# Up-projection start of a two-layer trunk: three chunks by halves of tokens in place of four, block 3's last steps by halves, and a moved weight split

## The chip, the cores and the metric

The kernel runs on one core of one Trainium2 chip. The metric is device time in microseconds (us) of one execution. TensorE is called PE here, VectorE DVE, ScalarE ACT, GpSimd POOL and SyncE SP, as in the profile.

## The reference, cut to what matters

The trunk has two layers on a residual stream `h` of 512 tokens by 1024 features, in float32. Each layer is a mixer (windowed attention in layer 0, forgetting attention in layer 1) and a ConvFFN, each with a norm before and a norm after. The change lies where the mixer's result is added and the ConvFFN begins:

```python
def rms_norm(x, g):
    x32 = x.astype(jnp.float32)
    y = x32 * lax.rsqrt(jnp.mean(x32 * x32, axis=-1, keepdims=True) + EPS)
    return (y * g.astype(jnp.float32)).astype(x.dtype)

def conv_ffn(xn, w_up, cw, cb, w_down):
    a = xn @ w_up                                   # 512 x 1024 by 1024 x 5632
    ap = jnp.pad(a, ((0, 0), (CONV_W - 1, 0), (0, 0)))
    a = sum(ap[:, j:j + T] * cw[j] for j in range(CONV_W)) + cb
    gate, val = jnp.split(a, 2, axis=-1)
    return (jax.nn.gelu(gate, approximate=True) * val) @ w_down
...
    h = h + rms_norm(mix, g[1])
    f = conv_ffn(rms_norm(h, g[2]), w_up[l], conv_w[l], conv_b[l], w_down[l])
    h = h + rms_norm(f, g[3])
```

## The kernel before, in words

**Precision.** Every product of a weight and an activation is made of three matmuls: each operand is split into a high part, rounded to the matmul's input type, and a low part, the difference. `mm3` (L290) issues high by high, high by low, low by high; these are the lines L291, L292 and L293 of the profile. Each has 128 rows of features on the partitions and 512 or 256 tokens as columns.

**Weights.** The class `Weights` brings the weights in pieces of 128 x 1024 through raw buffers. `load` issues the DMA on SP. `high` copies the piece to its high part on ACT (L60), `low` subtracts that from the raw piece on DVE (L78). `get` hands out the next piece and first splits ahead, up to `W.ahead` pieces counting from the one handed out. A few pieces are split in another way, with a DMA that adds (`high_added`, L98). As every engine works through its instructions in program order, the place at which a split is called is its place in the queues of ACT and DVE, and the place of the load it asks for in SP's.

**Order.** The schedule is written out by hand: an engine's order is the program's order, and waits between engines come from the data and the buffers. Eight PSUM banks are shared by everything that PE writes.

**The boundary.** The tokens lie in four blocks of 128. `Proj.finish` ends the mixer's projection block by block, in two halves of 512 features. After each half `Mix.part` squares the result on ACT (L333), multiplies it by its gain on DVE (L340), and after the second half takes the root. `Mix.add` (L342) takes the reciprocal and adds the block to `h` on DVE (L347). `Boundary.norm` then normalises `h`: `rstd_h` squares a whole block on ACT (L298), takes the root (L300) and the reciprocal (L304), and `normed` makes `xn` in two halves on DVE (L312). `transpose_in` transposes `xn` on PE in two groups of four (L362), ACT casts each group to the high part (L369), DVE makes the low part (L370). Blocks 0 and 1 pass through these steps inside the projection; `first_products` does block 3's norm and the transposes of blocks 2 and 3.

**The up-projection's start.** A chunk is 128 of the 5632 up-projected features; its weight is one piece. `first_products(bd, 4)` takes four chunks. The low half of the tokens (`LO`, blocks 0 and 1) of each is multiplied first, and between these products stand the transposes of block 2 (behind chunk 0) and block 3 (behind chunk 2). Then come the high halves (`HI`) of all four. Splits of three further pieces are called from here: ahead of chunks 1, 2 and 3, as `W.ahead` is 4 and four pieces are split at the start.

**After it.** `sums_in` prepares sums and differences of the transposed activations: two additions of 128 x 2048 on POOL (L670), called right behind `first_products`, then subtractions on DVE (L672 to L676) and splits on ACT and DVE (L681, L682). `post(0, ...)` and `post(1, ...)` do the convolution's taps of chunks 0 to 3, as pairs 0 and 1 (ACT L635, DVE L636 and L638), the gate (ACT L656) and the product of gate and value (DVE L653). The number in `post` and in the later loop counts pairs of a gate chunk and a value chunk. Pairs 2 and 3 go through `up`, with all 512 tokens in one matmul. From pair 4 on, most pairs are multiplied by a scheme with seven products of half size (`SEVEN`), which uses `sums_in`'s results; in it DVE reads a PSUM bank (L978, L982) before PE adds the next product to that bank. In layer 0, three small operations on DVE for a later gate weight (L1492 to L1494) stand between the end of `finish` and block 3's norm.

Of the kernel before, what the change touches and what calls it, by code (L numbers as in the profile page):

```python
# [11 lines left out]
BF16 = mybir.dt.bfloat16  # L12
AF = mybir.ActivationFunctionType
ALU = mybir.AluOpType

D = 1024
T = 512
NB = 4
KD = D // 128
# [3 lines left out]
EPS = 1e-6  # L23
# [94 lines left out]
def trunk_kernel(ctx, tc, x, norm_gains, w_qkv_a, w_o_a, w_q_b, w_o_b, kv_norm, w_kvf, b_f,  # L118
                 w_up, conv_w, conv_b, w_down, rope, out):
    nc = tc.nc  # L120
    act, dve, pool, pe, sp = nc.scalar, nc.vector, nc.gpsimd, nc.tensor, nc.sync
# [8 lines left out]
    def t8(shape, dt=F32, name="t8"):  # L130
        return p8.tile(shape, dt, tag="t8", name=name)

    def t4(shape, dt=F32, name="t4"):
        return p4.tile(shape, dt, tag="t4", name=name)

    def t2(shape, dt=F32, name="t2"):
        return p2.tile(shape, dt, tag="t2", name=name)

    def bank(shape, name="bank"):
        return psp.tile(shape, F32, tag="ps", name=name)  # L140

    def small(n, name):
        return sml.tile([128, n], F32, tag=name, name=name)
# [73 lines left out]
    W = Weights(nc, new_raw, lambda: t8([128, 2, 1024], F32R, name="w"), pieces)  # L217
# [4 lines left out]
    h = cst.tile([128, NB, D], F32, name="h")  # L222
# [6 lines left out]
    def load_gain(src, name):  # L229
        t = t4([128, D], name=name)  # L230
        sp.dma_start(t, bass.AP(tensor=src.tensor, offset=src.offset, ap=[[0, 128], [1, D]]))
        return t
# [57 lines left out]
    def mm3(o, ah, al, bh, bl, first, last, shared=False):  # L290
        pe.matmul(o, ah, bh, start=first, stop=False, skip_group_check=shared)  # L291
        pe.matmul(o, ah, bl, start=False, stop=False, skip_group_check=shared)  # L292
        pe.matmul(o, al, bh, start=False, stop=last, skip_group_check=shared)  # L293

    def rstd_h(b, between=None):
        ss = small(1, "s1")
        junk = t2([128, D], BF16, name="junk")
        act.activation(junk, h[:, b, :], AF.Square, scale=1.0 / 32, accum_out=ss)  # L298
        sd = small(1, "sd")
        act.activation(sd, ss, AF.Sqrt, bias=eps_t)  # L300
        if between is not None:
            between()
        r = small(1, "rs")
        dve.reciprocal(r, sd)  # L304
        return r

    H2 = (slice(0, 512), slice(512, 1024))

    def normed(b, r, gain):
        xn = t4([128, D], name="xn")  # L310
        for s, g in zip(H2, gain):
            dve.scalar_tensor_tensor(xn[:, s], h[:, b, s], r, g, ALU.mult, ALU.mult)  # L312
        return xn

    def by_half(gain):
        return [gain[:, s] for s in H2]

    class Mix:
# [5 lines left out]
        def half(self, b, n, hf, o):  # L324
            self.part(b, n, o, H2[hf], n == 1)
# [46 lines left out]
    def xs(xT, kc, s):  # L372
        return xT[0][kc // 4][:, kc % 4, s], xT[1][kc // 4][:, kc % 4, s]


    def feat_mm(w, xT, o, s):
        wh, wl = (t.rearrange("p (k c) -> p k c", k=8) for t in w)
        for kc in range(KD):
            bh, bl = xs(xT, kc, s)
            mm3(o[:, s], wh[:, kc, :], wl[:, kc, :], bh, bl, kc == 0, kc == KD - 1)  # L380
# [53 lines left out]
    class Boundary:  # L434
# [11 lines left out]
        def half(self, i, n, hf, o):  # L446
            b = self.order[i]
            self.mix.half(b, n, hf, o)
            if n == 0:
                if i >= 2:  # L450
                    self.transpose(self.order[i - 2])
                if i >= 1:
                    self.norm(self.order[i - 1])
            else:
                self.mix.add(b)

        def norm(self, b):
            self.r[b] = rstd_h(b)
            self.xn[b] = normed(b, self.r[b], by_half(self.gain_next))

        def transpose(self, b):
# [85 lines left out]
    def first_products(bd, n):  # L547
        bd.norm(3)
        outs = [bank([128, T], name="first") for _ in range(n)]
        ws = []  # L550
        for i, o in enumerate(outs):
            ws.append(W.get())
            feat_mm(ws[i], bd.xT, o, LO)
            if i == 0:
                bd.transpose(2)
            if i == 2:
                bd.transpose(3)
        for w, o in zip(ws, outs):
            feat_mm(w, bd.xT, o, HI)
        return outs  # L560
# [65 lines left out]
    def ffn(l, bd, cp, nxt, ahead):  # L626
# [39 lines left out]
        def sums_in():  # L666

            v = [t8([128, 4, T], name=f"xsum{i}") for i in range(2)]
            for i in range(2):
                pool.tensor_tensor(v[i], xT[0][i].bitcast(F32), xT[1][i].bitcast(F32), ALU.add)  # L670
            yield
            dve.tensor_tensor(v[0][:, :, LO], v[0][:, :, HI], v[0][:, :, LO], ALU.subtract)  # L672
            dve.tensor_tensor(v[0][:, :, HI], v[1][:, :, HI], v[0][:, :, HI], ALU.subtract)
            yield
            dve.tensor_tensor(v[1][:, :, HI], v[1][:, :, HI], v[0][:, :, LO], ALU.subtract)
            dve.tensor_tensor(v[1][:, :, LO], v[1][:, :, LO], v[1][:, :, HI], ALU.subtract)  # L676
            yield
            for X, src in ((XA, v[0]), (XB, v[1])):
                X += [t8([128, 4, T], F32R, name="xsh"), t8([128, 4, T], F32R, name="xsl")]
                for k in (0, 2):  # L680
                    act.copy(X[0][:, k:k + 2], src[:, k:k + 2])  # L681
                    dve.tensor_tensor(X[1][:, k:k + 2], src[:, k:k + 2], X[0][:, k:k + 2].bitcast(F32), ALU.subtract)  # L682
                    yield
# [250 lines left out]
        def up(w, o, kcs):  # L934
            wh, wl = (t.rearrange("p (k c) -> p k c", k=8) for t in w)
            for kc in kcs:
                bh, bl = xs(xT, kc, ALL)
                mm3(o, wh[:, kc, :], wl[:, kc, :], bh, bl, kc == 0, kc == KD - 1)

        base = W.n_get  # L940
        first = first_products(bd, 4)
        xT = bd.xT
        extra = sums_in()
        next(extra)
        post(0, first[0:2])
# [8 lines left out]
        for c in range(2, NF):  # L954
# [68 lines left out]
            else:  # L1023
                banks = [bank([128, T], name="up") for _ in range(1 if begun else 2)]
                if begun:
                    w, first = begun
# [165 lines left out]
    sd = tc.dram_tile([T, 8], F32, name="sd")  # L1192
# [291 lines left out]
    bd = Boundary(load_gain(norm_gains[0, 1], "gain01"), load_gain(norm_gains[0, 2], "gain02"), "xb")  # L1484
# [13 lines left out]

    bd2 = SharedBoundary(load_gain(norm_gains[0, 3], "gain03"), gcol, "xk")
    ffn(0, bd, cp[0], bd2, 4)  # L1500


# [67 lines left out]
    first, second = bd2.order[:2], bd2.order[2:]  # L1570
# [212 lines left out]
    for n in range(N + 3):  # L1783
        live = n < N
        if live:
            j, i = units[n]
# [51 lines left out]
    bd = Boundary(load_gain(norm_gains[1, 1], "gain11"), load_gain(norm_gains[1, 2], "gain12"), "xc")  # L1838
    po.finish(bd, 4)


    ffn(1, bd, cp, Final(load_gain(norm_gains[1, 3], "gain13")), 0)


# [40 lines left out]
```

## Time and profile before

| what | value |
|---|---|
| median of three runs | 1099.43 us (1098.59 to 1100.11) |
| the profiled execution's own time | 1098.99 us |
| its span, first to last instruction | 1097.2 us |
| mean granted clock of PE | 0.999 |
| PE busy | 1089.6 us, 99% |
| DVE busy | 878.0 us, 80% |
| ACT busy | 668.9 us, 61% |
| POOL busy | 175.9 us, 16% |

The profile is of one execution. A row of a timeline has the start in us from the span's start, the duration in us, the engine, the line of the kernel, the operation, the tiles written and read, shapes and types, and the count of instructions put together; in brackets stands how long the engine sat idle just before it, and what released it. A matmul's duration reaches over those that follow it, so PE's pace is read from the distance of starts. Rows of waits have the sum in us, the number of times and the longest.

In layer 0 the four chunks run from 173.18 to 197.93 us, in layer 1 from 751.98 to 776.73 us.

### The profile page before, as it was taken

What the parts mean: (1) busy time and instruction counts of PE and PEld (TensorE: products, weight loads), DVE (VectorE), ACT (ScalarE), POOL (GpSimd) and SP (SyncE); (2) the same over time, 40 slices, a digit from 0 to 9 for tenths busy, and PEclk for the clock granted to TensorE, in tenths of its full rate; (3) what the DMA queues carried; (4) which work ended last, traced back from release to release, by engine and by line L of the source; (5) the groups of instructions that cost most, each with busy time, mean ns of one, the idle gap of its engine ahead of it and who ended that gap; (6) DMA issues with size and microseconds to landing.
All of it is one profiled execution on the core that took longest, in us unless ns stands there. A gap on an engine that the chain in (4) does not pass through costs nothing.

```text
span 1097.2 us, 18058 instructions
## 1 busy us (share of the span) xinstructions
PE 1089.6 (99%) x6592; PEld 949.0 (86%) x6592; DVE 878.0 (80%) x1498; ACT 668.9 (61%) x1114; POOL 175.9 (16%) x245
## 2 busy tenths in 40 slices
PE   9999999999999999999999999999999999999997
PEld 7988889899999988888878888889899999988886
DVE  5898978887878689897686667858888778689894
ACT  6754665756666756576451577755756666647572
POOL 3633002211111111000001212101311111211000
PEclk9999999999999999999999999999999999999999
DMA  9699954567897979793447867774477978989872
GB/s 318 205 363 409 350 134 135 124 172 196 191 213 187 243 266 321 272 338 104 142 147 235 273 177 207 240 240 135 96 181 188 214 188 184 241 265 328 298 250 77
DMA packets 192129, 242.66 MB, mean 221 GB/s; under 512 B 12848, under 2 KB 138792, under 8 KB 192040
## 3 DMA queue, kind: packets, MB, share of 16 engines
q1 hardware_dynamic: 176408, 189.33, 53.2%
q0 software_dynamic: 14944, 52.18, 20.7%
q8 instruction: 52, 0.85, 0.3%
q14 instruction: 37, 0.30, 0.1%
q10 hardware_dynamic: 688, 0.01, 0.0%
HBM read 172.37 MB, written 39.73 MB: 193 GB/s over the span
## 4 chain that ended last, share of the span: by engine, by line
PE 98%; DVE 1%; issue 0%; ACT 0%; DVEq 0%
PE up L291 13%; PE up L292 13%; PE up L293 13%; PE acc L291 9%; PE acc L293 9%; PE acc L292 9%; PE v_ps L291 2%; PE v_ps L293 2%; PE v_ps L292 2%; PE qk_ps L1337 2%; PE o_ps L1741 2%; PE pT_ps L1726 2%; PE first L291 1%; PE first L293 1%; PE first L292 1%; PE qk_ps L291 1%
## 5 line engine op out<-in xcount | busy, mean ns | idle before, releaser
L291 PE MATMUL acc<-w 128*128 128x512 f32 (+1 forms) x311 | 120.6, 388 | 0.3 <-DVE mix L340 0.3
L293 PE MATMUL acc<-w 128*128 128x512 f32 (+1 forms) x311 | 120.4, 387 | 0.0
L292 PE MATMUL acc<-w 128*128 128x512 f32 (+1 forms) x267 | 103.2, 387 | 0.0
L291 PE MATMUL up<-xsh,w 128*128 128x256 f32 x352 | 99.6, 283 | 0.0
L292 PE MATMUL up<-xsl,w 128*128 128x256 f32 x352 | 99.6, 283 | 0.0
L293 PE MATMUL up<-xsh,w 128*128 128x256 f32 x352 | 99.6, 283 | 0.0
L78 DVE TENSOR_TENSOR w<-wraw,w 128x1024 fp32r<-128x1024 f32 x62 | 82.4, 1346 | 20.5 <-ACT w L60 20.1
L635 ACT ACTIVATE bb<-up,conv 128x512 f32<-128x512 f32 x80 | 59.7, 776 | 58.8 <-DVE up L1022 48.0
L60 ACT CAST w<-wraw 128x1024 fp32r<-128x1024 f32 x81 | 83.6, 1055 | 17.6 <-PE v_ps L292 6.9
L291 PE MATMUL up<-xch,w 128*128 128x512 f32 (+1 forms) x276 | 93.6, 339 | 0.0
L292 PE MATMUL up<-xbl,w 128*128 128x512 f32 (+1 forms) x276 | 93.5, 339 | 0.0
L292 PE MATMUL up<-xcl,w 128*128 128x512 f32 (+1 forms) x276 | 93.5, 339 | 0.0
L291 PE MATMUL up<-xbh,w 128*128 128x512 f32 (+1 forms) x276 | 93.5, 339 | 0.0
L293 PE MATMUL up<-xbh,w 128*128 128x512 f32 (+1 forms) x276 | 93.4, 338 | 0.0
L293 PE MATMUL up<-xch,w 128*128 128x512 f32 (+1 forms) x276 | 93.4, 338 | 0.0
L291 PEld LDWEIGHTS acc<-w 128*128 128x128 f32 x311 | 58.4, 188 | 12.6 <-DVE mix L340 0.7
L293 PEld LDWEIGHTS acc<-w 128*128 128x128 f32 x311 | 58.4, 188 | 11.7
L291 PEld LDWEIGHTS up<-xsh,w 128*128 128x128 f32 x352 | 67.6, 192 | 0.0
L292 PEld LDWEIGHTS up<-xsl,w 128*128 128x128 f32 x352 | 67.6, 192 | 0.0
L293 PEld LDWEIGHTS up<-xsh,w 128*128 128x128 f32 x352 | 67.6, 192 | 0.0
L605 DVE TENSOR_TENSOR dsums<-dsums 128x512 f32<-128x512 f32 x88 | 62.2, 709 | 4.0 <-DMA dsums<-in_w_down_dram 1.8
L636 DVE SCALAR_TENSOR_TENSOR bb<-up,conv,bb 128x511 f32<-128x511 f32 x80 | 59.5, 744 | 6.8 <-ACT bb L635 6.8
(311 smaller groups left out, 3097.7 us busy)
## 6 DMA issues: line engine op xcount, KB each, us to landing
wraw<-in_w_up_dram SPq DMA_DIRECT2D x88, 512.0 KB
w<-wraw POOLq DMA_DIRECT2D x32, 512.0 KB, 6.4
dT<-dsums SPq DMA_DIRECT2D x28, 512.0 KB
w<-wsum POOLq DMA_DIRECT2D x24, 512.0 KB, 5.7
dsums<-in_w_down_dram SPq DMA_DIRECT2D x22, 512.0 KB
dsums<-in_w_down_dram SPq DMA_DIRECT2D x44, 256.0 KB
hD<-hc POOLq DMA_DIRECT2D x44, 256.0 KB, 7.1
dact<-hD SPq DMA_DIRECT2D x44, 256.0 KB
```

The lines of the kernel that those rows point to most:

```text
L60: (copy or self.nc.scalar.copy)(pair[:, 0], raw)
L78: self.nc.vector.tensor_tensor(pair[:, 1], raw, pair[:, 0].bitcast(F32), ALU.subtract)
L291: pe.matmul(o, ah, bh, start=first, stop=False, skip_group_check=shared)
L292: pe.matmul(o, ah, bl, start=False, stop=False, skip_group_check=shared)
L293: pe.matmul(o, al, bh, start=False, stop=last, skip_group_check=shared)
L605: dve.tensor_tensor(o, p, m, ALU.subtract)
L635: act.activation(bb[:, s, :], ps, AF.Identity, bias=cp[:, 3, ch:ch + 1], scale=cp[:, 2, ch:ch + 1])
L636: dve.scalar_tensor_tensor(bb[:, s, 1:], ps[:, :T - 1], cp[:, 1, ch:ch + 1], bb[:, s, 1:], ALU.mult, ALU.add)
L1337: pe.matmul(qk_banks[b], a[n == 2], w[n == 1][:, kc % 2, :], start=kc + n == 0, stop=kc + n == KD + 1)
L1726: pe.transpose(o[:, k0 + k, :], p[:, hh, k * 128:(k + 1) * 128], ident)
L1741: pe.matmul(o[64 * hh:64 * hh + 64, i * 128:(i + 1) * 128], Vt[hd // 8][:, k, (hd % 8) * 64:(hd % 8) * 64 + 64], pT[j, i, hh][:, k, :], st ...
```

## The change

Four edits, used by both layers.

- `first_products` is called with three chunks. The fourth chunk is multiplied behind it with all tokens at once, by `up`, in a bank taken at that point.
- Block 3's transposes stand behind chunk 1's low half, where they stood behind chunk 2's.
- `W.ahead` is lowered by one for the `get` of chunk 1 and raised again behind block 3's transposes. The first split called from here thus comes with chunk 2's `get`, together with the second; the third comes with the fourth chunk's `get`.
- For the last block of a `Boundary`, `Mix.add` adds in two halves of 512 features, and the new `rstd_halves` squares in two halves, with the root's bias made from the first half's sum on DVE.

```diff
@@ -305,6 +305,19 @@
+    def rstd_halves(b):
+        ss, v = small(2, "ss"), small(1, "vr")
+        for n in range(2):
+            junk = t2([128, 512], BF16, name="junk")
+            act.activation(junk, h[:, b, H2[n]], AF.Square, scale=1.0 / 32, accum_out=ss[:, n:n + 1])
+            if n == 0:
+                dve.tensor_scalar(v, ss[:, 0:1], EPS, None, ALU.add)
+        sd = small(1, "sd")
+        act.activation(sd, ss[:, 1:2], AF.Sqrt, bias=v)
+        r = small(1, "rs")
+        dve.reciprocal(r, sd)
+        return r
@@ -451,11 +464,13 @@
+            elif i == 3:
+                self.mix.add(b, H2)
             else:
                 self.mix.add(b)
 
         def norm(self, b):
-            self.r[b] = rstd_h(b)
+            self.r[b] = (rstd_halves if b == self.order[3] else rstd_h)(b)
@@ -549,12 +564,14 @@
         outs = [bank([128, T], name="first") for _ in range(n)]
         ws = []
         for i, o in enumerate(outs):
+            if i == 1:
+                W.ahead -= 1
             ws.append(W.get())
             feat_mm(ws[i], bd.xT, o, LO)
-            if i == 0:
-                bd.transpose(2)
-            if i == 2:
-                bd.transpose(3)
+            if i < 2:
+                bd.transpose(2 + i)
+            if i == 1:
+                W.ahead += 1
         for w, o in zip(ws, outs):
             feat_mm(w, bd.xT, o, HI)
         return outs
@@ -938,8 +955,10 @@
         base = W.n_get
-        first = first_products(bd, 4)
+        first = first_products(bd, 3)
         xT = bd.xT
+        first.append(bank([128, T], name="first"))
+        up(W.get(), first[3], range(KD))
```

## The prediction

> **What bounds the kernel now.** I read the page's busy shares first, then what TensorE (PE) waited for, then the timelines of PE, ScalarE (ACT), VectorE (DVE) and GpSimd (POOL) around the up-projections' start in layer 0 (from 173.18 us), and last the same places of layer 1, 578.8 us later.
>
> ```profile
> PE 1089.6 (99%) x6592; PEld 949.0 (86%) x6592; DVE 878.0 (80%) x1498; ACT 668.9 (61%) x1114; POOL 175.9 (16%) x245
> PE warm L246 <- DVE zero L241: 1.2, 1, 1.2
> PE acc L291 <- DVE mix L340: 0.3, 1, 0.3
> PE qk_ps L1337 <- ACT xah L1304: 0.2, 1, 0.2
> ```
>
> PE is busy 99% of the span, and its waits in the whole execution sum to 1.7 us, none of them near the change. So the kernel ends when PE's list ends. Two things count: PE work taken away, and any stall that appears. What PE has there:
>
> ```profile
> 173.18 0.28 PE L291 MATMUL first<-xbh,w 128*128 128x256 f32 x1
> 176.05 1.04 PE L362 MATMUL xt_ps<-ident,xn 128*128 128x128 f32 x8
> 176.84 0.36 PE L291 MATMUL first<-xbh,w 128*128 128x256 f32 x1
> 182.67 1.04 PE L362 MATMUL xt_ps<-ident,xn 128*128 128x128 f32 x8
> 183.46 0.36 PE L291 MATMUL first<-xbh,w 128*128 128x256 f32 x1
> 197.93 0.40 PE L291 MATMUL up<-xbh,w 128*128 128x512 f32 x1
> 200.00 0.39 PE L291 MATMUL up<-xbh,w 128*128 128x512 f32 x1
> 205.44 0.39 PE L291 MATMUL up<-xbh,w 128*128 128x512 f32 x1
> ```
>
> Durations of matmuls overlap, so spacing is the price. From 183.46 to 197.93 lie 120 matmuls of 256 columns, 0.12 us each. From 200.00 to 205.44 lie 24 of 512 columns (one whole chunk), 0.2267 us each. The order is low half of chunk 0, block 2's transposes (176.05), two low halves, block 3's transposes (182.67), a low half, four high halves.
>
> **The PE work.** One chunk's 48 half matmuls (48 x 0.12 = 5.76 us) become 24 whole ones (24 x 0.2267 = 5.44). That saves 0.32 us a layer, 0.64 us in two. All of it is on the path.
>
> The Trainium skill (TensorE: Matmul & The Clock Gate, section "Wait — 56ns, not 53.3ns?") has a matmul's spacing as columns over 2.4 GHz and about 2.5 ns. By it I would estimate 24 x 2.5 ns = 0.06 us a layer, 0.12 in all. The rows here show 13 ns, not 2.5, saved by each pair that becomes one, and I take the rows.
>
> **Block 3's chain against its earlier transposes.** With one chunk less ahead, block 3's transposes follow 24 matmuls behind 176.84 and no longer 48. They move from 182.67 to 182.67 - 24 x 0.12 = 179.79. What must be ready by then:
>
> ```profile
> 173.38 0.60 ACT L333 ACTIVATE junk<-acc 128x512 bf16<-128x512 f32 x1 [0.59 <-PE acc L293]
> 176.46 1.06 ACT L298 ACTIVATE junk<-h 128x1024 bf16<-128x1024 f32 x1 [2.06 <-DVE h L347]
> 177.42 0.19 ACT L298 ACTIVATION_READ_ACCUMULATOR junk<-h 128x1 f32 x1
> 177.64 0.29 ACT L300 ACTIVATE sd<-s,eps_t 128x1 f32<-128x1 f32 x1
> 183.31 1.08 ACT L369 CAST xbh<-xt_ps 128x512 fp32r<-128x512 f32 x2 [2.52 <-PE xt_ps L362]
> 175.14 1.28 DVE L347 SCALAR_TENSOR_TENSOR h<-mix,rs,h 128x1024 f32<-128x1024 f32 x1
> 176.68 0.29 DVE L1494 TENSOR_TENSOR wfp<-wf,wfp 128x128 fp32r<-128x128 f32 x1
> 177.97 0.16 DVE L304 RECIPROCAL rs<-sd 128x1 f32<-128x1 f32 x1 [1.00 <-ACT sd L300]
> 178.17 1.41 DVE L312 SCALAR_TENSOR_TENSOR xn<-h,rs,gain 128x512 f32<-128x512 f32 x2
> 183.93 1.29 DVE L370 TENSOR_TENSOR xbl<-xt_ps,xbh 128x512 fp32r<-128x512 f32 x2 [0.88 <-ACT xbh L369]
> ```
>
> Today the addition (175.14), squares, root, reciprocal and the two halves of xn follow each other, and xn is complete at 178.17 + 1.41 = 179.58. That is only 0.2 us ahead of 179.79. By halves, the first addition (half of the 1.41 that a pair of 128x512 costs) ends at 175.85 and the second at 176.55. The squares cost 0.60 each by the row of 173.38 and a read of 0.19: the first runs beside the second addition, the second from 176.6, with its read done at 177.3. The new small operation on DVE stands behind the gate weights' operations (done at 176.97) and ends at about 177.3 too. Then root, reciprocal, xn: 177.3 + 0.3 + 0.2 + 1.41 puts xn at 179.25. Gain 0.3 us, and half a microsecond in hand at the transposes. I charge nothing. If the pieces did not overlap at all (addition 1.41 for 1.28, squares 0.33 dearer, the small operation 0.15), xn would come at 180.2 and PE would stall 0.4 us a layer: a rival below.
>
> Behind the transposes, ACT's casts start 0.64 us later (183.31 against 182.67) and DVE's differences 0.62 us after those, so 180.43 and 181.05, done by 182.4. The first high half starts at 179.79 + 0.79 + 2.96 = 183.54. No wait.
>
> **The weights' splits.** Lowering the look-ahead for one step puts both splits that ran between the two blocks' transposes behind block 3's, on ACT and on DVE; a third follows as before. For PE that is harmless: these weights serve matmuls from 197.6 on. But DVE then does all three differences while POOL adds up the transposed activations:
>
> ```profile
> 184.70 10.19 POOL L670 TENSOR_TENSOR xsum<-xbh,xbl 128x2048 f32<-128x2048 f32 x2 [76.70 <-DVE xbl L370]
> 184.70 4.62 POOL L670 TENSOR_TENSOR xsum<-xbh,xbl 128x2048 f32<-128x2048 f32 x1 [76.70 <-DVE xbl L370]
> 180.70 2.35 DVE L78 TENSOR_TENSOR w<-wraw,w 128x1024 fp32r<-128x1024 f32 x2
> 185.36 5.04 DVE L78 TENSOR_TENSOR w<-wraw,w 128x1024 fp32r<-128x1024 f32 x1
> 190.32 0.74 DVE L636 SCALAR_TENSOR_TENSOR bb<-first,conv,bb 128x511 f32<-128x511 f32 x1
> 191.09 0.75 DVE L638 SCALAR_TENSOR_TENSOR bb<-first,conv,bb 128x510 f32<-128x510 f32 x1
> 193.19 0.75 DVE L636 SCALAR_TENSOR_TENSOR bb<-first,conv,bb 128x511 f32<-128x511 f32 x1 [1.35 <-ACT bb L635]
> 194.64 1.34 DVE L672 TENSOR_TENSOR xsum<-xsum 128x1024 f32<-128x1024 f32 x1
> 99.39 0.77 POOL L1116 TENSOR_TENSOR rope<-qk,rope 128x64 f32<-128x64 f32 x1
> 105.33 0.32 POOL L1116 TENSOR_TENSOR rope<-qk,rope 128x64 f32<-128x64 f32 x1
> 99.90 1.54 DVE L82 SCALAR_TENSOR_TENSOR w<-wraw,gcol,w 128x512 fp32r<-128x512 f32 x2
> ```
>
> The first two differences took 2.35 us as a pair. The third, started 0.66 us into POOL's first addition, took 5.04 and ended at 190.40, 1.08 us behind that addition's end (184.70 + 4.62 = 189.32). POOL's second addition took the other 5.57 us, a microsecond more than the first. So these two engines exclude each other when DVE's both inputs are in SBUF. The taps at 190.32, with one input in a PSUM bank, ran at full speed beside POOL. Who goes next after a hand-over? Around 99.4 us, while DVE sent such operations one after the other (the pair at 99.90), POOL's small products took 0.77 us each against 0.32 without them, but each came through behind one DVE operation. They took turns.
>
> After the change POOL's first addition starts 2.03 us behind the transposes, as today: 181.82 to 186.44. The first difference (its cast ready at about 182.5) ends 1.08 later, 187.52. POOL's second addition, already asked for, then holds until 181.82 + 10.19 = 192.01. The second difference ends at 193.09, the third 1.14 later at 194.23. The taps of pair 0 begin at 194.15 in place of 190.32, 3.83 us late. They then run without the idle 1.35 us, and L672 at 1.23 in place of 1.34. So DVE is 3.83 - 1.35 - 0.11 = 2.37 us late from there on, and ACT, which alternates with it, too.
>
> The Trainium skill (SBUF — State Buffer, section "Who interferes with whom") calls the port that DVE and GpSimd share an exclusive lock, held for a whole instruction by whichever issued first, and counts a DVE instruction with two SBUF inputs against a GpSimd one that reads SBUF. By the first rows alone (one difference blocked, the hand-over unknown) the sum could stay at -0.64; by the page, POOL's second addition issued ahead of the second difference and goes first, as in my sum.
>
> Does PE notice? The first consumer that is tight is pair 4, where PE adds into a bank that DVE must have read first (L978):
>
> ```profile
> 221.08 0.75 DVE L638 SCALAR_TENSOR_TENSOR bb<-up,conv,bb 128x510 f32<-128x510 f32 x1
> 222.86 0.42 DVE L978 TENSOR_TENSOR csum<-up,csum 128x256 f32<-128x256 f32 x1 [1.03 <-PE up L293]
> 224.03 0.28 PE L291 MATMUL up<-xsh,w 128*128 128x256 f32 x1
> 800.15 0.75 DVE L638 SCALAR_TENSOR_TENSOR bb<-up,conv,bb 128x510 f32<-128x510 f32 x1
> 801.66 0.42 DVE L978 TENSOR_TENSOR csum<-up,csum 128x256 f32<-128x256 f32 x1 [0.76 <-PE up L293]
> 802.83 0.28 PE L291 MATMUL up<-xsh,w 128*128 128x256 f32 x1
> SPq L50 <- DVE w L78: 2.6, 2, 1.9
> ```
>
> Layer 0: DVE is free at 221.08 + 0.75, less an overlap of 0.08, = 221.75 now, 224.12 then; L978 ends at 224.54. PE wants that bank at 224.03 - 0.32 = 223.71. Stall 0.83 us. Layer 1: 800.82 + 2.37 + 0.42 = 803.61 against 802.51, stall 1.10. Sum 1.93. Behind it DVE has waits of its own on PE, so I let the delay end there. Two weight loads on SP wait for these differences to free their raw buffers (last row, 2.6 us now); they are issued later with the differences, but their data is first used behind the taps of pairs 0 and 1, which stand in the same delayed list. I charge nothing; were one late, it would show as a wait on a DMA.
>
> **Sum.** 1098.99 us (the profiled execution: span 1097.2 and 1.8 around it) - 0.64 + 1.93 = 1100.3. That execution lies 0.44 below the median 1099.43, on which the forecast is set: 1100.7.
>
> **The rivals.** (a) DVE keeps the port through its three differences. Then they end at 187.5, 188.7 and 189.9, before today's 190.40, POOL's second addition ends at 194.5 against today's 194.89, nothing is late: 1099.43 - 0.64 = 1098.8. For it: the next difference is already in DVE's queue. Against: the turns at 99.4 us. (b) Slower: the whole 3.83 us arrives at L978, since ACT, bound to DVE's order, gives back none of the 1.35. Stalls 2.29 and 2.56, so 1099.43 + 4.85 - 0.64 = 1103.6. It decides from a delay of about 2.9 us on, where the net loss passes 2.2. Against: both inputs of those taps are ready long before. (c) xn comes at 180.2: 0.4 us a layer more on PE, all else moving with it: 1101.5. (d) The halves do nothing, because 179.58 was early enough: then nothing here changes, the time is the forecast's. That is within it.
>
> **How the numbers follow.** 0.2%, 2.2 us, is about what a measurement of this kernel can tell from no change. Forecast 0.57, (a) 0.20, (b) 0.13, (c) 0.10. Faster by over 2.2 us has no mechanism, as PE had no stall here to lose; 0.03 for what I overlook, out of (a). The forecast's own spread is 1099.2 to 1102.2, 0.10 of it above 1101.6; with (b) and half of (c) slower gets 0.28, and 0.69 remains within. The range 1098.4 to 1103.0 takes in (a) and (c) and leaves out most of (b).
>
> **What would show it.** Right: block 3's transposes at about 179.8 with no wait, three L78 differences of which two take about 5 us, taps of pair 0 at about 194, and a PE wait on L978 of about a microsecond in each layer. Wrong: L78 at 5, 1.2 and 1.2 us and no PE wait (a); PE waiting for xn (c); waits over 2 us at L978 (b); or a wait on a DMA.

## The result, and the profile after

The changed kernel's median is 1101.74 us (1100.78 to 1102.42, 14 runs), beside 1099.88 us (1098.59 to 1101.2, 14 runs) of the kernel before: ratio 1.0017, 95% interval 1.001 to 1.0025. That is 1.9 us, or 0.17%, slower (1.1 to 2.8), within the 0.2% named in the prediction. Its profiled execution took 1102.42 us, span 1100.5.

Lines below line 308 have moved in the changed kernel: L670 is now L687, L312 L325, L362 L375, L636 L653, L672 L689, L978 L997, L982 L1001. The first half matmul of layer 0 starts at 173.82 us and not at 173.18. The profiles of one and the same kernel differ there by some tenths, so times below are compared by their distance from that matmul.

The page's first line and PE's waits, the latter as total, times and longest (PEld is PE's loading of weights):

```profile
PE 1091.2 (99%) x6544; PEld 946.9 (86%) x6544; DVE 886.5 (81%) x1502; ACT 669.6 (61%) x1118; POOL 175.0 (16%) x245
PE up L291 <- DVE csum L997: 1.5, 2, 0.8
PE warm L246 <- DVE zero L241: 1.2, 1, 1.2
PE up L293 <- DMA w<-wraw: 0.4, 1, 0.4
PE acc L291 <- DVE mix L353: 0.3, 1, 0.3
```

PE has 48 matmuls fewer (24 a layer). Two waits are new: twice on the sum that the prediction named, once on an adding DMA. DVE is 8.5 us busier, which is mostly weight differences that stand and wait: three of them are 11.76 us of one row below, and were 2.35 + 5.04 us before. The timeline around the chunks:

```profile
173.82 0.28 PE L291 MATMUL first<-xbh,w 128*128 128x256 f32 x1
178.51 1.41 DVE L325 SCALAR_TENSOR_TENSOR xn<-h,rs,gain 128x512 f32<-128x512 f32 x2
180.43 1.03 PE L375 MATMUL xt_ps<-ident,xn 128*128 128x128 f32 x8
182.46 10.21 POOL L687 TENSOR_TENSOR xsum<-xbh,xbl 128x2048 f32<-128x2048 f32 x2 [73.82 <-DVE xbl L383]
183.12 11.76 DVE L78 TENSOR_TENSOR w<-wraw,w 128x1024 fp32r<-128x1024 f32 x3
192.81 0.40 PE L291 MATMUL first<-xbh,w 128*128 128x512 f32 x1
194.81 0.74 DVE L653 SCALAR_TENSOR_TENSOR bb<-first,conv,bb 128x511 f32<-128x511 f32 x1
197.69 1.22 DVE L689 TENSOR_TENSOR xsum<-xsum 128x1024 f32<-128x1024 f32 x1
198.28 0.39 PE L291 MATMUL up<-xbh,w 128*128 128x512 f32 x1
```

Block 3's `xn` is complete at 179.92, half a microsecond ahead of its transposes at 180.43, which do not wait. The whole chunk takes 198.28 - 192.81 = 5.47 us. The three differences take 11.76 us together. POOL's additions run from 182.46 to 192.67, so the first two differences stand beside them; the third comes after. And at pair 4:

```profile
224.67 0.41 DVE L997 TENSOR_TENSOR csum<-up,csum 128x256 f32<-128x256 f32 x1
225.14 0.39 PE L291 MATMUL up<-xsh,w 128*128 128x256 f32 x1 [0.62 <-DVE csum L997]
226.44 0.41 DVE L1001 TENSOR_TENSOR csum<-up,csum 128x256 f32<-128x256 f32 x1
226.91 0.39 PE L291 MATMUL up<-xbh,w 128*128 128x256 f32 x1
805.03 0.38 PE L291 MATMUL up<-xsh,w 128*128 128x256 f32 x1 [0.84 <-DVE csum L997]
820.88 0.50 PE L293 MATMUL up<-xch,w 128*128 128x512 f32 x1 [0.38 <-DMA w<-wraw]
239.96 0.40 PE L291 MATMUL up<-xbh,w 128*128 128x512 f32 x1
```

L997 ends at 225.08 and PE goes on at 225.14; L1001 ends at 226.85 and PE goes on at 226.91. The bracket shows only the idle part that a matmul's long duration leaves visible, so I take stalls from the distance of starts, less the usual distance (0.12 us for 256 columns). They are 0.78 and 0.24 us in layer 0, 1.00 and 0.24 in layer 1, and 0.55 at 820.88. Behind each of the first four, the next distance is 0.10 longer too.

The last row is the first matmul of pair 6. I call its distance from the first half matmul the stage: 239.96 - 173.82 = 66.14 us, and 66.37 in layer 1. Before it was 65.25 in both (238.43 - 173.18):

```profile
238.43 0.40 PE L291 MATMUL up<-xbh,w 128*128 128x512 f32 x1
```

So PE loses 0.89 us in layer 0 and 1.12 in layer 1, 2.01 together, against a measured 1.9.

### The profile page after: what moved, and what is told of

Same layout as the page of the kernel before. It is cut to its first block, busy times and chain, and to the rows that moved or that the text cites. A ratio compares the mean times of both kernels' runs of the same rounds, so it can differ in the third digit from the quotient of the medians.

```text
span 1100.5 us, 17973 instructions
## 1 busy us (share of the span) xinstructions
PE 1091.2 (99%) x6544; PEld 946.9 (86%) x6544; DVE 886.5 (81%) x1502; ACT 669.6 (61%) x1118; POOL 175.0 (16%) x245
## 4 chain that ended last, share of the span: by engine, by line
PE 93%; DVE 3%; issue 1%; ACT 1%; DMA 1%; DVEq 0%; POOLq 0%; ACTq 0%
PE up L293 11%; PE up L291 11%; PE up L292 11%; PE acc L291 9%; PE acc L293 9%; PE acc L292 9%; PE v_ps L291 2%; PE v_ps L293 2%; PE v_ps L292 2%; PE qk_ps L1356 2%; PE pT_ps L1745 2%; PE o_ps L1760 2%; PE s_ps L1711 2%; PE qk_ps L291 1%; PE q_ps L291 1%
## 5 line engine op out<-in xcount | busy, mean ns | idle before, releaser
L78 DVE TENSOR_TENSOR w<-wraw,w 128x1024 fp32r<-128x1024 f32 x62 | 90.9, 1487 | 21.3 <-ACT w L60 21.0
L653 DVE SCALAR_TENSOR_TENSOR bb<-up,conv,bb 128x511 f32<-128x511 f32 x80 | 59.5, 744 | 7.7 <-ACT bb L652 7.6
```

Source lines behind the costliest of these rows:

```text
L78: self.nc.vector.tensor_tensor(pair[:, 1], raw, pair[:, 0].bitcast(F32), ALU.subtract)
L653: dve.scalar_tensor_tensor(bb[:, s, 1:], ps[:, :T - 1], cp[:, 1, ch:ch + 1], bb[:, s, 1:], ALU.mult, ALU.add)
```

## The experiments

The theory is the prediction's: the differences meet POOL's two additions, DVE falls behind, PE waits at pair 4. The rivals are that the splits' later place by itself, the whole chunk or the order of the banks, or the halves make the loss.

**e1, the splits alone.** On the kernel before, four chunks by halves:

```diff
+            if i in (1, 2):
+                W.ahead -= 1
             ws.append(W.get())
 ...
             if i == 2:
                 bd.transpose(3)
+                W.ahead += 2
```

> The kernel before, with one part of the change alone: four chunks by halves, whole additions and squares, block 3's transposes where they were, but all three weight splits behind them. Theory (POOL's two additions hold up DVE's weight differences): the second and third difference now also meet POOL, the third ends at about 197.1 us of the old clock in place of 190.4, DVE stays about 5.2 us late, and PE waits for L978 about 3.4 us in layer 0 and 3.7 us in layer 1: about 7 us slower, 1107. Rival 1 (splits merely come later, each at its own 1.2 us): no wait, within 0.5 us of before. Rival 2 (the loss comes from the whole chunk or the order of the PSUM banks): neither is in this kernel, so within 0.5 us of before.

Ratio 1.0076 (1.0063 to 1.0089), 8.4 us slower for the forecast 7. DVE, then PE at pair 4, then a row of the windows (length, busy time and count of PE, PEld, DVE, ACT and POOL, PE's granted clock, DMA share, GB/s):

```profile
185.77 11.74 DVE L78 TENSOR_TENSOR w<-wraw,w 128x1024 fp32r<-128x1024 f32 x3
197.44 0.74 DVE L639 SCALAR_TENSOR_TENSOR bb<-first,conv,bb 128x511 f32<-128x511 f32 x1
222.64 0.39 PE L293 MATMUL up<-xsh,w 128*128 128x256 f32 x1 [0.68 <-DMA w<-wsum]
227.76 0.39 PE L291 MATMUL up<-xsh,w 128*128 128x256 f32 x1 [2.22 <-DVE csum L981]
227.90:231.30 3.40, 3.40 (x17) 3.40 (x18) 3.37 (x6) 0.26 (x2) 0.00 (x0) 0.53 0.24 71
```

The loss is there without the whole chunk and without the halves, so neither is needed for it. The taps start 23.84 us behind the first half matmul (at 173.60); in the theory the third difference ends 197.1 - 173.18 = 23.92 us behind it, and taps start 0.08 us ahead of that. PE's stalls in layer 0 are 0.83 us and 2.38 us (L981), together 3.2 for the forecast 3.4; in layer 1 they are 1.06 and 2.46, together 3.5 for 3.7. The first of each pair is on a DMA that adds a low part: it landed as fast as in the kernel before (6.9 us for 6.6 in layer 0) but was issued 5.1 us later in the stage, because its input came late. The stage is 4.91 and 5.12 us longer in this profile, though, as the granted clock fell to 0.53 for some 3.4 us behind the second stall of each layer. That was not in the expectation.

**e2, POOL waits.** On the changed kernel:

```diff
+            pool.tensor_copy(v[0][:, 0, 0:1], W.ready[W.n_split - 1][1][:, 0:1].bitcast(F32))
             for i in range(2):
                 pool.tensor_tensor(v[i], xT[0][i].bitcast(F32), xT[1][i].bitcast(F32), ALU.add)
```

> The changed kernel, with one tiny POOL copy that reads the third split's low part ahead of POOL's two additions, so that these start when DVE's differences are done. Nothing else moves. Theory: the three differences take 1.2 us each, the taps of pair 0 start about 6 us earlier than in the changed kernel, POOL's second addition ends about 0.5 us later than in the kernel before, no PE wait at L978; the saving of 0.64 us is left: 0.6 us faster than before, some 2.5 us faster than the changed kernel. Rival 1 (the splits' place in the queues of ACT and DVE, not POOL) and rival 2 (whole chunk, bank order): as the changed kernel, about 1.9 us slower than before.

Ratio 0.9989 (0.9980 to 0.9998). DVE and POOL:

```profile
183.37 3.50 DVE L78 TENSOR_TENSOR w<-wraw,w 128x1024 fp32r<-128x1024 f32 x3
186.99 0.19 POOL L686 COPY xsum<-w 128x1 f32<-128x1 f32 x1 [78.10 <-DVE w L78]
187.25 9.19 POOL L688 TENSOR_TENSOR xsum<-xbh,xbl 128x2048 f32<-128x2048 f32 x2
```

The same splits in the same places take 3.50 us and not 11.76, and POOL's additions 9.19 and not 10.21. Within the stage PE has no wait. The stage is 64.93 in both layers, 0.32 shorter than before, which is the saving of the whole chunk to the hundredth. The loss is POOL's meeting with the differences; the splits' place is not.

**e3, two splits behind the taps.** Only the first split stays ahead of them:

```diff
-            if i == 1:
-                W.ahead += 1
 ...
         first.append(bank([128, T], name="first"))
+        W.ahead -= 1
         up(W.get(), first[3], range(KD))
 ...
         post(0, first[0:2])
+        W.split(base + 7)
         next(extra)
```

> The changed kernel with only the first of the three splits ahead of the taps of pair 0 and the two others behind these taps, where DVE would have to wait for POOL anyway. Theory: one difference of 5 us as before the change, taps from about 187.5 us of the old clock, second and third difference done by about 194.3, no PE wait at L978: 0.6 us faster than before. Rival 1 (the later the splits the worse): slower than the changed kernel. Rival 2: as the changed kernel, 1.9 us slower than before.

Ratio 0.9998 (0.9989 to 1.0006). The stage is 64.93 in both layers, as the theory has it, and the splits stand later than in any other kernel here:

```profile
182.29 5.04 DVE L78 TENSOR_TENSOR w<-wraw,w 128x1024 fp32r<-128x1024 f32 x1
193.00 2.36 DVE L78 TENSOR_TENSOR w<-wraw,w 128x1024 fp32r<-128x1024 f32 x2 [1.35 <-ACT w L60]
PE up L293 <- DMA w<-wsum: 1.6, 1, 1.6
```

The time does not show the forecast 0.6 us. In this profile PE waits 1.6 us for an adding DMA 211 us after the stage of layer 1 began, and some 0.6 us for two others.

**e4, no halves.** `rstd_h` for block 3, and `Mix.add` whole:

> The changed kernel without its halves: block 3 is added and squared whole, as before. By the prediction xn is then complete 0.2 us ahead of block 3's transposes in place of 0.5: no PE wait for xn, time within 0.2 us of the changed kernel (1.9 us slower than before). Rival (the halves are needed): a PE wait for xn of 0.1 to 0.5 us a layer.

Ratio 1.0016 (1.0007 to 1.0025), the stage 66.12 and 66.40: the changed kernel's, within a few hundredths.

```profile
178.08 1.41 DVE L325 SCALAR_TENSOR_TENSOR xn<-h,rs,gain 128x512 f32<-128x512 f32 x2
179.71 1.04 PE L375 MATMUL xt_ps<-ident,xn 128*128 128x128 f32 x8
```

`xn` is complete 0.22 us ahead of its transposes. With the splits where the change puts them, the halves hide nothing.

**e5, no edit of the look-ahead** (the two `W.ahead` steps taken out):

> The changed kernel without its edit of the look-ahead: the first of the three splits stands between the transposes of block 2 and block 3 again, the two others behind block 3's. Theory: only two differences meet POOL, the third ends about 1.2 us earlier than in the changed kernel, DVE is about 1.2 us late in place of 2.4, and its idle time ahead of L978 (1.03 us in layer 0, 0.76 in layer 1, and 0.7 until PE needs the bank, less the 0.32 that PE is early) takes that up: no PE wait at L978 over 0.1 us, block 3's differences about 0.6 us later but still ahead of the first high half; 0.6 us faster than before. Rival (any split behind the transposes costs in proportion): half the changed kernel's loss, 0.6 us slower than before. Rival (the split had to move, or block 3's transposes wait): a PE wait for xn or for block 3's differences.

Ratio 1.001 (1.0001 to 1.0019), 1.1 us slower and not 0.6 faster.

```profile
180.84 1.22 DVE L78 TENSOR_TENSOR w<-wraw,w 128x1024 fp32r<-128x1024 f32 x1
183.17 10.84 DVE L78 TENSOR_TENSOR w<-wraw,w 128x1024 fp32r<-128x1024 f32 x2
PE up L293 <- DMA w<-wraw: 0.9, 1, 0.9
```

One difference is early, two meet POOL, and L978's counterpart stops PE for no more than 0.11 us, as expected. But the stage is 65.45 and 65.47, 0.42 us longer together in place of 0.64 shorter. The main reason is the next wait: the product after that (on `o1`) starts only when L982's counterpart has read the other half of the same bank, 0.24 us late in each layer, and each of the two restarts costs a tenth. The rest is the DMA wait, 1.07 us by the starts, at pair 6 of layer 1.

**e6, neither look-ahead edit nor halves:**

> The changed kernel without its edit of the look-ahead and without its halves: three chunks by halves, the fourth whole, and the earlier transposes of block 3 are all that is left. Theory: xn 0.2 us ahead of the transposes, block 3's differences end just before the first high half needs them; PE waits of at most 0.3 us a layer, 0.1 to 0.6 us faster than before. Rival (halves and split are needed together): PE waits for xn or for block 3's differences of half a microsecond a layer or more.

Ratio 1.0022 (1.0013 to 1.0031), slower than forecast.

```profile
PE up L293 <- DMA w<-wsum: 1.9, 1, 1.9
PE up L293 <- DMA w<-wraw: 0.8, 1, 0.8
PE up L291 <- DVE csum L991: 0.8, 2, 0.5
```

There is no wait at block 3's transposes. Its differences come later behind the early split, POOL starts later, and DVE's list ends 0.3 us later than in e5 (stage 65.78 and 66.05), enough to stop PE at both sums. So the halves do buy 0.9 us on PE when one split is early, through DVE's list and not through the transposes. In this profile two DMA waits add 3 us by the starts, and the forecast had none.

**e7, two chunks by halves**, on top of e2:

> The changed kernel with the waiting POOL copy of the earlier run, and with two chunks by halves in place of three (the third and fourth whole). PE saves 0.32 us more a layer, but the first high half follows block 3's transposes at once: its second matmul needs the first low part, about 2.0 us behind the transposes' start, and could start 0.9 us behind it. Theory (the cover between transposes and high halves is what a chunk by halves buys): a PE wait of about 1.1 us a layer behind block 3's transposes, 0.8 us slower than before, 1.5 us slower than with three chunks and the copy. Rival (the casts and differences keep up): 0.6 us faster than with three chunks and the copy.

Ratio 1.0009 (1.0000 to 1.0018); the forecast was 0.8 us slower.

```profile
180.56 0.38 PE L291 MATMUL first<-xbh,w 128*128 128x256 f32 x1 [0.24 <-ACT xbh L382]
181.29 0.39 PE L292 MATMUL first<-xbl,w 128*128 128x256 f32 x1 [0.34 <-DVE xbl L383]
190.53 5.62 DVE L690 TENSOR_TENSOR xsum<-xsum 128x1024 f32<-128x1024 f32 x1 [0.94 <-POOL xsum L688]
```

The first high half waits for block 3's cast, its second matmul for the difference. The stage is 65.73 in both layers, 0.80 longer than e2's: 1.12 us of stalls, for the forecast 1.1, less the 0.32 saved. A difference of POOL's own sums (L690) starts just behind POOL's second addition, which runs to 195.06, and takes 5.62 us where it takes 1.22 in the changed kernel (L689 there): the same exclusion once more.

**The DMA wait at pair 6.** Its first weight is split by a DMA that adds. In the kernel before it landed 7.3 us behind its issue, in the changed one 9.1 and in e5 9.6; PE needed it 8.8 us behind the issue before, and 8.5 in the changed kernel and e5, whose stalls bring the issue 0.3 us closer to the need. Four kernels (e9 to e12) were profiled a second time as they were, and e8 splits that weight on DVE (`ADDED` without 6), on top of e2.

> The changed kernel with the waiting POOL copy (as earlier) and with one more edit: the first weight of pair 6 is split by a difference on DVE, where an adding DMA made its low part. In the profiles so far that DMA took 7.1 to 9.6 us to land and PE needed the result 8.8 us behind its issue; four kernels waited 0.4 to 1.1 us for it in layer 1. Theory (this wait took part of the saving): no PE wait at pair 6, PE's waits near the change all gone, 0.6 us faster than before. Rival (the wait is taken over by the longer list of DVE): a PE wait on DVE in pairs 4 to 6.

> The changed kernel unaltered, another profile. Theory: the waits on L978's counterpart (0.8 and 1.0 us in the first profile, with 0.2 in each layer at the next product) return to within 0.1 us, since they come from instruction order. The wait for the adding DMA at pair 6 of layer 1 (0.55 us) changes from execution to execution, anywhere from 0 to 1 us. Rival: it returns at 0.5 to 0.6 us, and is part of the change's cost.

> The changed kernel without its look-ahead edit, unaltered from the earlier run, another profile. Theory: again no wait at L978's counterpart and 0.2 us a layer at the next product; the DMA wait at pair 6 of layer 1 (1.07 us before) changes from execution to execution. Rival: it returns at about 1.1 us, and explains why this kernel was slower than forecast.

> The kernel before, unaltered, another profile. Theory: no PE wait near the change; at pair 6 of layer 1 a DMA wait of 0 to 0.3 us can appear, as the DMA landed 1.5 us ahead of need in the first profile. Rival (such DMA waits belong to every kernel here in equal measure): a wait of 0.5 us or more.

> The changed kernel with the waiting POOL copy, unaltered from the earlier run, timed again, because the kernel that differs from it by one weight's split (e8) was timed 0.7 us slower than before and not 0.6 faster. Theory: PE again has no wait on DVE or POOL in either layer, and reaches pair 6 in each layer 0.32 us sooner than before; the time is 0.6 us faster than before, give or take the interval's 0.9. Rival (the first timing was luck, DMA waits elsewhere take the saving back): same as before or slower, with DMA waits of half a microsecond or more in the profile.

| kernel | stage, layer 0 and 1 | DMA waits of PE in this profile | time in us, or ratio to before |
|---|---|---|---|
| e9, changed, again | 66.13, 66.44 | none | 1101.44 us, one run |
| e10, as e5, again | 65.44, 65.47 | none | 1099.79 us, one run |
| e11, before, again | 65.25, 65.25 | none | 1098.71 us, one run |
| e8, e2 without that DMA | 64.93, 64.93 | 0.5, elsewhere | 1.0007 (0.9998 to 1.0016) |
| e12, as e2, again | 64.93, 64.93 | none | 0.9995 (0.9986 to 1.0004) |

The stalls that come from the order of instructions return within 0.1 us, the stage within 0.07. The DMA waits do not: 0.55 and none in the changed kernel, 1.07 and none in e5. They belong to the execution: in the first profile of the changed kernel this DMA landed 7.3 us behind its issue in layer 0 and 9.1 in layer 1, and in the two profiles of the kernel before it landed 7.2 to 8.2 us behind it. The kernel before had none of these waits in two profiles, the altered ones had some in seven of eleven, without e1, whose wait came from a late input. Whether a changed order makes them likelier, or eleven profiles are only more than two, stays open. e2, which saves 0.64 us on PE, is the fastest here, but its two timings, 0.9989 and 0.9995, are at the edge of what can be told from no change, and e3 and e8, which save as much on PE, were not faster. Part of this spread lies ahead of the change. In the fourteen profiles the first half matmul comes at 172.68 to 174.07 us, and in the two of the kernel before at 172.86 and 173.18. Nearly all of that arises in the first ten us of the execution, where no kernel here differs from another; from there on the way to this matmul is the same within 0.25 us.

## Why the prediction was right, point by point

The forecast was 1100.7 us, 1.27 above the median that it was set on; measured 1101.74, 1.9 above its own comparison, in the range and in the likeliest case.

- **PE's saving** of 0.32 us a layer: shown by e2 and e12, exact. The whole chunk took 5.47 us for 5.44.
- **The other price of a matmul.** The 2.5 ns a matmul of the Trainium skill (TensorE: Matmul & The Clock Gate, section "Wait — 56ns, not 53.3ns?") would have made it an estimated 0.06 us a layer. The stages show 0.32, so the rows decided rightly.
- **Block 3's chain**: xn 0.5 us ahead, no wait; right. Rival (c) fell. Rival (d), that the halves do nothing, holds for the change as made (e4), though not with a split ahead of block 3's transposes (e6 against e5).
- **The differences**: the taps 20.99 us behind the first half matmul (194.81 - 173.82), forecast 20.97 (194.15 - 173.18). The turns that POOL and DVE took at 99.4 us decided the hand-over, and rival (a) fell. The Trainium skill's exclusive lock (SBUF — State Buffer, section "Who interferes with whom") agrees with the runs: e2 takes the two apart in time, and the differences take 3.50 us in place of 11.76.
- **The idle time given back**, and with it the delay of 2.37 us at L978: rival (b), the whole 3.83, fell. Stalls there 0.78 and 1.00 us for 0.83 and 1.10.
- **Where it was short**: the step "I let the delay end there". The next product waits for L982's counterpart, 0.24 us a layer, although it writes another half of the bank than the one read; and each of two restarts a layer costs 0.10 us. That is 0.9 us over both layers, of which the smaller stalls at L978 give back 0.15. By the stage the sum is +2.0 and not +1.3. But for the restart, the rows of the kernel before would have given it:

```profile
224.65 0.41 DVE L982 TENSOR_TENSOR csum<-up,csum 128x256 f32<-128x256 f32 x1
225.47 0.28 PE L291 MATMUL up<-xbh,w 128*128 128x256 f32 x1
```

L978 ends at 223.28 and L982 at 225.06, 1.78 us later. Between them DVE does two taps without idle time, where the prediction counted on waits of its own. The product that PE restarts with takes 225.47 - 224.03 = 1.44 us, and 0.10 more behind a stall. So a PE that was held at L978 comes 1.78 - 1.54 = 0.24 us too early for L982, which is what the changed kernel shows.

- **What was overlooked**: the waits for adding DMAs, which differ between executions by up to a microsecond each. The prediction has a wait on a DMA among its signs of being wrong, and the first profile shows one of 0.55 us, behind the stage; in the second (e9) it is gone and the stage is the same.
- **Two slips in the working**, without effect on the forecast: 177.3 + 0.3 + 0.2 + 1.41 is 179.21 and not 179.25, and by the prediction's own stalls the net loss passes 2.2 us from a delay of 2.8 us on, not 2.9.

## What to carry to other kernels

Before moving work behind a point, look what another engine starts at that point: here DVE's differences were harmless in both places as work, and two of them took over four times as long beside POOL (10.84 us for two in e5, where the early one took 1.22). When an engine falls behind, add up its idle times up to the first consumer with little room, and then look at the next consumer too, since a list without idle time delays all that follow. A saving of a third of a microsecond a layer is read from the starts of instructions, not from the time of whole runs, where waits for DMAs and the first ten us vary by as much.

## What the runs showed that was not expected

A stall of 2.4 us on PE, some 5 us behind one of 0.8 (e1), was followed by about 3.4 us at a granted clock of 0.53, in which 256 columns took 0.21 us each and not 0.12. That cost some 1.5 us a layer, half as much again as the stalls. The stalls of about a microsecond in the changed kernel left the clock alone. The Trainium skill (TensorE: Matmul & The Clock Gate, section "What's actually happening") has the clock halved after at least one idle window of about 3.4 us. Here no idle time of PE was that long, and the clock fell all the same, in both layers; the measurement decides.

A product into one half of a PSUM bank waited for DVE's reading of the other half in all six profiles in which that reading was late (the changed kernel, e4 to e6, e9 and e10). The trace shows the wait as one that the program asks for, on the product's first weight load (L1001 ends at 226.85):

```profile
226.91 0.19 PEld L291 LDWEIGHTS up<-xbh,w 128*128 128x128 f32 x1 [0.28 <-DVE csum L1001]
```

Whether the chip would do without this wait was not tried.
